# RWKV pairs in a hybrid trunk: products per head on 64x64 array parts, and the chunk inverse by 8x8 columns and doubling

## The chip, the cores and the metric

One core of a Trainium2 chip runs the whole program. Its engines work side by side, each through its own queue in order: TensorE (PE in the profile, with its weight loads as PEld), VectorE (DVE), ScalarE (ACT), GpSimd (POOL) and SyncE (SP, which issues the DMAs). The metric is the device time of one execution in microseconds (us). The kernel before takes 2580.99 us, the median of three runs (2580.29 to 2584.45).

## The reference

Two layers over 256 tokens of width 2048. Each adds a mixer and then a feed-forward part to the residual stream. Layer 0 mixes with HGRN2 and RWKV7, layer 1 with mLSTM and Mamba2. The change touches the RWKV7 part alone, 16 heads of 64 channels:

```
def rwkv7_scan(r, w, k, v, kk, a):
    def step(state, inp):
        rt, wt, kt, vt, kkt, at = inp
        sa = jnp.einsum('bhvk,bhk->bhv', state, -kkt)
        state = (state * wt[:, :, None, :] + sa[..., :, None] * (kkt * at)[:, :, None, :]
                 + vt[..., :, None] * kt[:, :, None, :])
        return state, jnp.einsum('bhvk,bhk->bhv', state, rt)
...
    o_rw = rwkv7_scan(rh, heads(decay), kh, vh, kk, heads(a))
    o_rw = head_layernorm(o_rw, rw_ln_w, rw_ln_b, RW_GN_EPS)
    bonus = (jnp.sum(rh * kh * rw_r_k, axis=-1, keepdims=True) * vh).reshape(b, s, RW_WIDTH)
    o_rw = (o_rw + bonus) * gate
```

The kernels don't step through tokens. They take chunks of 64: with the decays folded into the operands, a chunk's corrections `sa` for all its tokens solve a triangular system, so that the inverse of (I - M) is wanted, where M is a strictly triangular 64x64 matrix of products between the chunk's tokens, one for each head and chunk.

## The kernel before

The **large products** of all layers (the bulk) split each f32 operand in a high and a low part in a faster format and take three products of parts. `weights` (L275) loads a weight tile `raw`, ScalarE casts it to `whi` and VectorE subtracts to get `wlo`, with three tiles of each kind on chip. `bulk_a` (L293) has 512 columns moving, `bulk_b` (L319) 256. Both write to banks called `b`; all small products write to banks called `m`.

In **layer 0**, `flow` (L344) traces the bulk and, beside it, chains of small steps, as Python generators. In each round each active chain takes one step (two RWKV pairs and one HGRN2 head at a time), and then the bulk takes three steps (`EVEN_RATIO`), each of three to six products. What is traced in this order goes to the engines' queues, where the scheduler may still shift some of it. `ORDER` (L35) says in which order the bulk computes the inputs of the eight RWKV pairs and of HGRN2's parts, and the bulk of pair p waits until pair p - 3 is done (`AHEAD`). The chains' products have plain f32 operands; each such product is two instructions on TensorE in the profile. Transposes (`tr`, L135) are one.

A **pair** (`rwkv_pair`, L608) is two heads over four chunks of 64 tokens, all its tiles in one of two memory regions called `lane`. A matrix over a chunk's tokens that is a stationary operand stands block-diagonal, [128, 128] with the two heads' 64x64 blocks, half of it zero. VectorE makes those by masks (`masked`, L694; and `fh`, `sh` for B and K). In order, with a `yield` (the next step of the chain) between most of these:

- norms, decays and their exponentials; `vt` is v transposed for each chunk
- B and K block-diagonal, A and R side by side in `AR`
- `gram` (L687) twice: B and K as stationary operands against A and R, 128 columns moving; then `mt` copied by ScalarE, and the masks `m4`, `mrb`, `mak`, `mrk` by VectorE
- the inverse's diagonal blocks of 4 by Horner's rule (L719): three steps of four products with 4 columns moving. Between them `kt` (K transposed), `rv` and `o0` (products with v)
- four doublings, m = 4, 8, 16, 32 (L748): `halves` masks M's part (`lm`) and the inverse so far (`w`); TensorE transposes `w` and multiplies `lm` with x, ScalarE copies both results; in a second step TensorE multiplies them, and VectorE joins the halves. With m = 4 goes `kv`, with m = 8 `bt` (B transposed)
- the whole inverse made block-diagonal, transposed and copied to `xT`
- the scan over the four chunks, the only part whose products were per head before: `both` (L593) takes the two heads in turns on array parts of 64x64, at the lower and upper 64 partitions. The product with `xT` (L806) uses the full array
- layer norm, the transposes to `oc`, and the product with the gate

Of the kernel before, what the change touches and what calls it, by code (L numbers as in the profile page):

```python
# [16 lines left out]
ALU = mybir.AluOpType  # L17
# [8 lines left out]
# Blocks of 128 rows that a step over the weights takes, steps in one transfer and such transfers on chip where there  # L26
# is room for larger ones, and each kind of weight tile's number on chip.
# [13 lines left out]
PAIR_KB = dict(bon=0, AR=1, mrb=3, vt=4, B=5, K=7, mt=9, m4=11, mak=13, mrk=15, kt=17, kk=9, sqk=10, invw=11, k2=12,  # L41
               kka=13, b=14, E=15, rv=13, o0=15, kv=17, bt=5, lm=7, w=8, xh=11, y=14, x64=16, xw=9, xT=11, u=8, sq=7,
               oc=14)
PAIR_COL = dict(inv=0, gap=4, sm=8, var=12, x40=16, x41=32, x8=48, x16=80, x32=144, sd=272, st0=336, st1=400,
                rhs0=464, rhs1=528)
LANE = 19 * 256 + 592
# [16 lines left out]
class Arena:  # L63
    """Tiles that stay, one after the other in a few large ones."""
# [15 lines left out]
class Trunk:  # L80
# [42 lines left out]
    def rsqrt(self, x, scale, eps):  # L123
        """(x * scale + eps) ** -0.5 in place, for a few columns."""
        self.ts(x, x, scale, ALU.mult, eps, ALU.add)
        n = x.shape[-1]
        self.nc.gpsimd.tensor_tensor(out=x, in0=x, in1=self.nhalf[:, 0:n], op=ALU.pow)
# [29 lines left out]
    def even_masks(self, c):  # L157
# [5 lines left out]
        self.b4 = self.t(c, [P, P], "b4")  # L163
        for tl, m in ((self.bd, 64), (self.b4, 4)):
            nc.gpsimd.memset(tl, 1.0)
            self.same_block(tl.rearrange("p (j r) -> p j r", r=m), m, m)
        self.lev = {}
        for m in (1, 2, 4, 8, 16, 32, 64):
            nb = P // (2 * m)
# [6 lines left out]
        self.low = {}  # L176
        for m in (4, 8, 16, 32):
            tl = self.t(c, [P, 64 // m, m], f"low{m}")
            nc.gpsimd.memset(tl, 1.0)
            self.same_block(tl, 2 * m, m, m)  # L180
            self.low[m] = tl

    def even_masks_2(self, c):
        nc = self.nc
        self.upi = self.t(c, [P, 2, 64], "upi")
        self.ups = self.t(c, [P, 2, 64], "ups")
        self.up4 = self.t(c, [P, 2, 64], "up4")
        flat = lambda x: x.rearrange("p h t -> p (h t)")
        self.mul(flat(self.upi), self.up, self.bd)
        self.sub(flat(self.ups), flat(self.upi), self.ident)  # L190
        self.mul(flat(self.up4), flat(self.ups), self.b4)
        red = lambda o, x: nc.vector.tensor_reduce(out=o, in_=x, axis=AX.X, op=ALU.add)
        self.id4 = self.t(c, [P, 4], "id4")
        red(self.id4, self.ident.rearrange("p (j n) -> p n j", n=4))
        self.half_upi = self.t(c, [P, 64], "hupi")
        nc.vector.tensor_copy(out=self.half_upi[0:64], in_=self.upi[0:64, 0, :])
        nc.vector.tensor_copy(out=self.half_upi[64:128], in_=self.upi[64:128, 1, :])
        # 1 on the first (second) halves of blocks of 2m, as columns
        self.fh, self.sh = {}, {}
        for m in (4, 8, 16, 32, 64):  # L200
            f, g = self.t(c, [P, 1], f"fh{m}"), self.t(c, [P, 1], f"sh{m}")
            red(f, self.lev[m])
            self.ts(f, f, 1.0 / m, ALU.mult)
            self.ts(g, f, -1.0, ALU.mult, 1.0, ALU.add)
            self.fh[m], self.sh[m] = f, g
# [69 lines left out]
    def weights(self, src):  # L275
        """Parts of WK blocks of 128 rows of src [rows, n, c]: hi and lo as [128, WK, n * c]."""
# [7 lines left out]
    def weights_ahead(self, src, n, pool):  # L284
        """As weights, for n * WK blocks of src [rows, c] that come in one transfer."""
# [1056 lines left out]
```

## Time and profile before

| | |
|---|---|
| median of three runs | 2580.99 us |
| the profiled execution's span | 2578.8 us (nothing is profiled around it) |
| the pairs' chains, first to last | pair 0 begins at 123 us, pair 7 ends at 703 us |
| instructions of TensorE | 13969 |
| traffic with HBM | 424.35 MB read, 165 GB/s over the span |

The page of the profile gives each engine's busy time and its share of the span. Behind it stand views by stretch of time (windows), by line and form of instruction, the chain of waits that ended last, and the timeline of each engine. In the operands, `128*64` is the part of the array that a product uses, rows by columns, and `128x4` what moves through it. A matmul's end is modelled, so prices are read from one start to the next.

### The profile page before, as it was taken

The numbers are of one execution on the slowest core, as the hardware profiler recorded it, in microseconds if no ns is written. First come the engines' busy times: TensorE is split into PE (matmuls) and PEld (weight loads), VectorE is DVE, ScalarE is ACT, GpSimd is POOL, SyncE is SP. The second block draws the span as 40 slices with busy tenths as digits, with TensorE's granted clock in tenths as the row PEclk, the third lists the DMA queues.
The fourth block names the chain that finished last, engine by engine and source line by source line (L and its number), as shares of the span: only waits on it lengthen the run. The fifth ranks groups of instructions, "written<-read, shape, count | busy, mean of one in ns | idle before, by whom it ended". The sixth has DMA issues, their size and how long they took to land.

```text
span 2578.8 us, 35284 instructions
## 1 busy us (share of the span) xinstructions
PE 2543.4 (99%) x13969; PEld 2166.6 (84%) x13969; DVE 1499.9 (58%) x2327; ACT 1191.1 (46%) x1651; POOL 51.0 (2%) x106
## 2 busy tenths in 40 slices
PE   7999999999999999999999999999999999999998
PEld 5898899988788888888888899988888888888886
DVE  3567767766664454545454678656654544455455
ACT  5456556543354434444344555454544434443443
POOL 2000000000000000000000000000000000000000
PEclk9999999998999999999999999999999999999999
DMA  4633533232465555555555465567455555555554
GB/s 147 180 104 110 148 100 99 76 113 82 151 217 181 195 189 192 190 189 187 196 189 187 119 185 149 164 178 238 155 183 193 194 190 188 192 185 194 195 182 145
DMA packets 271094, 428.75 MB, mean 166 GB/s; under 512 B 18363, under 2 KB 86193, under 8 KB 270801
## 3 DMA queue, kind: packets, MB, share of 16 engines
q1 hardware_dynamic: 270353, 425.45, 52.3%
q8 instruction: 110, 1.80, 0.3%
q10 hardware_dynamic: 576, 1.05, 0.1%
q14 instruction: 55, 0.45, 0.0%
HBM read 424.35 MB, written 2.10 MB: 165 GB/s over the span
## 4 chain that ended last, share of the span: by engine, by line
PE 96%; DVE 2%; ACT 1%; DMA 1%; issue 0%; POOL 0%; SPq 0%; POOLq 0%; ACTq 0%; DVEq 0%
PE b L130 84%; PE m L130 8%; PE m L135 3%; DVE wlo L109 1%; PE m L597 1%; DMA act<-x 0%; ACT whi L269 0%; DMA raw<-w_in_even 0%; ACT xs L121 0%; ACT act L121 0%; DVE xs L103 0%; DVE act L109 0%; DVE act L106 0%; DVE act L112 0%; DVE cy L112 0%
## 5 line engine op out<-in xcount | busy, mean ns | idle before, releaser
L130 PE MATMUL b<-whi,act 128*128 128x512 f32 x5376 | 1687.1, 392 | 0.6
L109 DVE TENSOR_TENSOR wlo<-raw,whi 128x1024 fp32r<-128x1024 f32 (+2 forms) x818 | 978.0, 1198 | 862.5 <-ACT whi L269 855.5
L269 ACT CAST whi<-raw 128x1024 fp32r<-128x1024 f32 (+2 forms) x818 | 839.3, 1027 | 1128.2 <-PE b L130 1059.0
L130 PEld LDWEIGHTS b<-whi,act 128*128 128x128 f32 x5376 | 1010.6, 188 | 210.2 <-DVE act L109 1.9
L130 PE MATMUL b<-wlo,act 128*128 128x512 f32 x2688 | 1049.0, 390 | 0.0
L130 PEld LDWEIGHTS b<-wlo,act 128*128 128x128 f32 x2688 | 505.8, 188 | 103.2 <-DVE wlo L109 0.5
L130 PE MATMUL b<-act,whi 128*128 128x256 f32 (+1 forms) x2048 | 394.6, 290 | 0.3 <-ACT act L269 0.3
L130 PEld LDWEIGHTS b<-act,whi 128*128 128x128 f32 (+1 forms) x2048 | 319.1, 191 | 3.1 <-ACT act L269 0.7
L130 PE MATMUL b<-act,wlo 128*128 128x256 f32 (+2 forms) x1024 | 291.9, 288 | 1.0 <-DVE wlo L109 0.7
L130 PEld LDWEIGHTS b<-act,wlo 128*128 128x128 f32 (+2 forms) x1024 | 194.0, 191 | 2.7 <-DVE wlo L109 1.9
L130 PEld LDWEIGHTS m<-lane 128*128 128x128 f32 (+2 forms) x1024 | 115.5, 183 | 14.4 <-issue 7.8
L130 PE MATMUL m<-lane 128*128 128x64 f32 (+10 forms) x1024 | 123.2, 257 | 0.4 <-ACT lane L770 0.3
L106 DVE TENSOR_TENSOR act<-act,b 128x512 f32<-128x512 f32 x96 | 62.2, 682 | 11.0 <-PE b L130 11.0
L121 ACT ACTIVATE he<-he 128x256 f32<-128x256 f32 (+1 forms) x120 | 47.6, 408 | 22.1 <-DVE he L109 19.1
L135 PE MATMUL m<-const,lane 128*64 128x128 f32 (+2 forms) x304 | 45.3, 272 | 0.8 <-DVE lane L103 0.8
L103 DVE TENSOR_TENSOR lane<-lane,masks 128x256 f32<-128x256 f32 (+1 forms) x72 | 32.3, 451 | 14.9 <-PE m L130 13.9
L130 PE MATMUL m<-he 128*128 128x64 f32 (+1 forms) x240 | 38.3, 280 | 1.1 <-DVE he L103 1.1
L121 ACT ACTIVATE sg<-b,rs 128x512 f32<-128x512 f32 x44 | 29.9, 688 | 19.9 <-PE b L130 19.8
L135 PEld LDWEIGHTS m<-const,lane 128*64 128x64 f32 (+2 forms) x304 | 32.3, 126 | 6.6 <-issue 2.1
L130 PEld LDWEIGHTS m<-he 128*128 128x128 f32 x240 | 32.3, 193 | 3.0 <-ACT he L121 1.3
L103 DVE TENSOR_TENSOR he<-he,act 128x128 f32<-128x128 f32 x128 | 32.3, 288 | 3.1 <-ACT he L121 2.8
L112 DVE SCALAR_TENSOR_TENSOR gu<-b,rs,sg 128x512 f32<-128x512 f32 x44 | 30.9, 743 | 0.0
(243 smaller groups left out, 1104.3 us busy)
## 6 DMA issues: line engine op xcount, KB each, us to landing
raw<-ffn_w_up SPq DMA_DIRECT2D x176, 1024.0 KB
raw<-ffn_w_down SPq DMA_DIRECT2D x88, 1024.0 KB
raw<-w_in_odd SPq DMA_DIRECT2D x88, 512.0 KB
raw<-w_in_even SPq DMA_DIRECT2D x192, 128.0 KB
raw<-w_in_even SPq DMA_DIRECT2D x32, 512.0 KB
raw<-w_in_even SPq DMA_DIRECT2D x64, 256.0 KB
raw<-w_out_even SPq DMA_DIRECT2D x32, 512.0 KB
raw<-w_out_odd SPq DMA_DIRECT2D x32, 512.0 KB
```

Of the source, the lines that this page charges most:

```text
L103: self.nc.vector.tensor_tensor(out=out, in0=a, in1=b, op=ALU.mult)
L106: self.nc.vector.tensor_tensor(out=out, in0=a, in1=b, op=ALU.add)
L109: self.nc.vector.tensor_tensor(out=out, in0=a, in1=b, op=ALU.subtract)
L112: self.nc.vector.scalar_tensor_tensor(out=out, in0=a, scalar=s, in1=b, op0=op0, op1=op1)
L121: self.nc.scalar.activation(out=out, in_=a, func=f, **k)
L130: self.nc.tensor.matmul(out, lhsT, rhs, start=start, stop=stop)
L135: self.nc.tensor.transpose(out=out, in_=in_, identity=self.ident[b:b + k, b:b + k])
L269: self.nc.scalar.copy(out=hi, in_=src)
L597: self.nc.tensor.matmul(out[s], lhsT[s], rhs[s], start=start, stop=stop)
```

## The change

Nothing outside `rwkv_pair`, its masks and its places in memory is changed. In a pair:

- B, K and all masked matrices are [128, 4, 64]: a head's block on its own 64 partitions, nothing block-diagonal. VectorE makes B and K by one product each in place of two; the mask products go over 256 columns in place of 512, but there are seven (three for the doublings, `lm8`, `lm16`, `lm32`, which `mt` and its later masks were before).
- All products of two heads go through `heads`, which is `both` for each chunk, on 64x64 parts. That holds for `gram`, `rv`, `o0`, `kv`, the doublings and the product with the inverse.
- `vt`, `bt`, `kt` and `oc` are turned by products with the identity on 64x64 parts (`turned`), two instructions each, where they were transposes. ScalarE copies each of the first three once, where `vt` and `bt` took two copies; VectorE reads `oc` from its bank.
- Horner's rule is gone. The diagonal blocks of 8 are folded to 8 columns by a reduction; VectorE's `stream_shuffle` spreads the entries of columns 1 to 6 in each block of 8 partitions, and six pairs of small products and sums build the inverse of all 8x8 blocks.
- Three doublings are left. X and its transpose Y stand on 32 columns; `nc.vector.transpose` turns 32x32 blocks on VectorE. Each doubling has two products, X through M's level, then that through Y; VectorE adds to X, transposes to Y, and widens Y to 64 columns by a mask.
- A pair has 28 yields in place of 31.

The core of the diff:

```
-        B, K = T("B", BD), T("K", BD)
-        for o, x in ((K, k2), (B, kka)):
-            for h, sel in enumerate((self.fh[64], self.sh[64])):
-                self.stt(o[:, :, h, :], V4(x), sel, V4(E), ALU.mult, ALU.mult)
+        B, K = T("B"), T("K")
+        self.mul(K, k2, E)
+        self.mul(B, kka, E)
...
+    def heads(self, out, lhsT, rhs):
+        for ch in range(4):
+            self.both(out[:, ch, :], lhsT[:, ch, :], rhs[:, ch, :])
...
+        def turned(x, tag):
+            ps = quarter()
+            for ch in C4:
+                for h in range(2):
+                    s = slice(h * 64, (h + 1) * 64)
+                    self.mm(ps[s, ch, :], x[s, ch, :], self.ident[s, s])
+            if tag is None:
+                return ps
+            o = T(tag, CM)
+            nc.scalar.copy(out=o, in_=ps)
+            return o
...
-        for i in range(3):
-            ps = self.bank()[:, 0:16].rearrange("p (c n) -> p c n", n=4)
-            for ch in C4:
-                self.mm(ps[:, ch, :], m4[:, ch, :], self.id4 if x is None else x[:, ch, :])
-            x = T(f"x4{i % 2}", (P, 4, 4))
-            self.add(x, ps, i4)
...
+        z = T("m8", (P, 4, 8))
+        nc.vector.tensor_reduce(out=z, in_=m8e.rearrange("p c (j n) -> p c n j", n=8), axis=AX.X, op=ALU.add)
+        sh, tmp = T("sh", (P, 6, 4, 8)), T("tmp", (P, 4, 8))
+        for n in range(1, 7):
+            nc.vector.stream_shuffle(out=sh[:, n - 1].rearrange("p c n -> p (c n)"), in_=z.rearrange("p c n -> p (c n)"),
+                                     mask=[i // 8 * 8 + n for i in range(32)])
+        rv = times_v(mak, "rv")
+        yield
+        for n in range(1, 7):
+            w = 7 - n
+            self.mul(tmp[:, :, 0:w], sh[:, n - 1, :, n + 1:8], z[:, :, n:n + 1].broadcast_to([P, 4, w]))
+            self.add(z[:, :, n + 1:8], z[:, :, n + 1:8], tmp[:, :, 0:w])
+        self.add(z, z, by4(self.id8))
+        o = times_v(mrk, "o0")
+        yield
...
-        for m in (4, 8, 16, 32):
-            lm, w = halves(m)
...
-            ps = self.bank()[0:64].rearrange("p (c t) -> p c t", t=P)
-            for ch in C4:
-                self.tr(ps[:, ch, :], w[:, ch, :])
-            xT = T("xh", (64, 4, P))
-            nc.scalar.copy(out=xT, in_=ps)
...
+        nc.vector.transpose(out=flat(X), in_=flat(Y))
+        widened()
+        Yf = Y64.rearrange("p c j n -> p c (j n)")
+        for m in (8, 16, 32):
+            if m == 8:
+                kv = times_v(kt, "kv")
+            yield
+            ps = self.bank()[:, 0:P].rearrange("p (c n) -> p c n", n=32)
+            self.heads(ps, mt[m], X)
+            y = T("y", (P, 4, 32))
+            nc.scalar.copy(out=y, in_=ps)
+            yield
+            ps = self.bank()[:, 0:P].rearrange("p (c n) -> p c n", n=32)
+            self.heads(ps, Yf, y)
+            if m < 32:
+                self.add(X, X, ps)
+                nc.vector.transpose(out=flat(Y), in_=flat(X))
+                widened()
             else:
...
-            self.mm(pu, xT[:, ch, :], rhs)
+            self.both(pu, Yf[:, ch, :], rhs)
```

TensorE's queue around the two steps of pair 0's second doubling (m = 8) before: `m_1554` and `m_1560` are the transposes of `w` and the products of `lm`, `b_` the bulk.

```order
L130 MATMUL b_1536<-act_105,whi_1538 128x256
L130 MATMUL b_1536<-act_104,wlo_1539 128x256
L135 MATMUL m_1554<-const_58,lane_106_621 64x128 x4
L130 MATMUL m_1560<-lane_106_621 64x8 x4
L130 MATMUL b_1535<-act_104,whi_1538 128x256
L130 MATMUL b_1535<-act_105,whi_1538 128x256
```

And pair 0's second doubling (m = 16) in the changed kernel; `m_1569` is M's level times X, two heads by four chunks.

```order
L130 MATMUL b_1551<-act_105,whi_1553 128x256
L130 MATMUL b_1551<-act_104,wlo_1554 128x256
L586 MATMUL m_1569<-lane_106_606 64x32 x8
L130 MATMUL b_1550<-act_104,whi_1553 128x256
L130 MATMUL b_1550<-act_105,whi_1553 128x256
```

The transposes have left TensorE's queue, and a stretch of eight products on 64x64 parts stands alone between bulk products.

VectorE's queue from pair 0's Gram products to its first doubling, before: `m_1316` and `m_1324` are the Gram banks, the rows with 128x16 the sums of Horner's steps, `wlo` the bulk's weights.

```order
L103 TENSOR_TENSOR lane_106_621<-m_1316,masks_105_599 128x512
L103 TENSOR_TENSOR lane_106_621<-m_1316,masks_105_599 128x256
L103 TENSOR_TENSOR lane_106_621<-m_1324,masks_105_599 128x512 x2
L106 TENSOR_TENSOR lane_106_621<-m_1356,masks_105_599 128x16
L103 TENSOR_TENSOR lane_106_621<-lane_106_621,masks_249 128x256
L109 TENSOR_TENSOR wlo_1482<-raw_1480,whi_1481 128x1024
L106 TENSOR_TENSOR lane_106_621<-m_1393,masks_105_599 128x16
L109 TENSOR_TENSOR wlo_1539<-raw_1537,whi_1538 128x2x384
L106 TENSOR_TENSOR lane_106_621<-m_1430,masks_105_599 128x16
```

The same place in the changed kernel (`m_1302`, `m_1316` are the Gram banks now):

```order
L103 TENSOR_TENSOR lane_106_606<-m_1302,masks_105_593 128x256 x5
L103 TENSOR_TENSOR lane_106_606<-m_1316,masks_105_593 128x256 x2
L716 TENSOR_REDUCE lane_106_606<-lane_106_606 128x32
L719 STREAM_SHUFFLE lane_106_606<-lane_106_606 128x32 x6
L103 TENSOR_TENSOR lane_106_606<-lane_106_606 128x4x6
L106 TENSOR_TENSOR lane_106_606<-lane_106_606 128x4x6
L103 TENSOR_TENSOR lane_106_606<-lane_106_606 128x4x5
L106 TENSOR_TENSOR lane_106_606<-lane_106_606 128x4x5
L103 TENSOR_TENSOR lane_106_606<-lane_106_606 128x4x4
L106 TENSOR_TENSOR lane_106_606<-lane_106_606 128x4x4
```

Between these steps VectorE no longer takes results of TensorE: all of it follows from the Gram banks, one instruction after the other, with no weight tile of the bulk between them.

More of the change, by code (lines that the diff above doesn't have):

```diff
@@ L38 @@
 ODD_RATIO = 3.0
[L41 to L46, printed above, removed]
+PAIR_KB = dict(bon=0, AR=1, mrb=3, vt=4, u=4, B=5, rv=5, K=6, o0=6, kk=7, bt=7, k2=8, kt=8, sq=8, kka=9, mak=9, oc=9,
+               E=10, mrk=10, sqk=11, invw=11, m8e=11, Y=11, b=12, lm8=12, lm16=13, lm32=14, kv=15, X32=16, Y32=16.5,
+               y=17)
+PAIR_COL = dict(inv=0, gap=4, sm=8, var=12, m8=16, tmp=48, sh=80, sd=272, st0=336, st1=400, rhs0=464, rhs1=528)
+LANE_KB = 17.5
+LANE = int(LANE_KB * 256) + 592
 EPS = 1e-6
@@ L175, in even_masks, with fold @@
             self.lev[m] = tl
-        self.low = {}
-        for m in (4, 8, 16, 32):
[L178 to L181, printed above, removed]
     def even_masks_2(self, c):
         nc = self.nc
[L185 to L205, printed above, removed]
+        up = self.t(c, [P, P], "up2")
+        def fold(tag, x, n):
+            o = self.t(c, [P, n], tag)
+            nc.vector.tensor_reduce(out=o, in_=x.rearrange("p (j n) -> p n j", n=n), axis=AX.X, op=ALU.add)
+            return o
+        self.mul(up, self.up, self.bd)
+        self.upi = fold("upi", up, 64)
+        self.sub(up, up, self.ident)
+        self.ups = fold("ups", up, 64)
+        self.mul(up, up, self.b8)
+        self.up8 = fold("up8", up, 64)
+        self.lev64 = {m: fold(f"lev64_{m}", self.lev[m], 64) for m in (8, 16, 32)}
+        self.id8 = fold("id8", self.ident, 8)
+        self.m8, self.m32 = fold("m8", self.e8, 4), fold("m32", self.e32, 2)
     def same_block(self, v, size, keep, first=0):
@@ L525, in even_layer @@
             self.masks()
-            self.even_masks(Arena(self.t(masks, [P, 1664], "masks")))
+            self.even_masks(Arena(self.t(masks, [P, 1428], "masks")))
             self.omu = self.t(self.const, [P, 27], "omu")
@@ L602, in pair_tile @@
     def pair_tile(self, lane, tag, shape=(P, S)):
[L603 removed]
+        at = int(PAIR_KB[tag] * 256) if tag in PAIR_KB else int(LANE_KB * 256) + PAIR_COL[tag]
         v = lane[0:shape[0], at:at + math.prod(shape[1:])]
@@ L684, in rwkv_pair @@
         yield
-        Bf, Kf, ARf = flat(B), flat(K), flat(AR)
+        B, K = V4(B), V4(K)
+        ARf = AR.rearrange("p c h t -> p c (h t)")
         def gram(lhs):
-            ps = self.bank().rearrange("p (c h t) -> p c h t", c=4, h=2)
-            for ch in C4:
-                self.mm(ps[:, ch].rearrange("p h t -> p (h t)"), lhs[:, ch, :], ARf[:, ch, :])
-            return ps[:, :, 0, :], ps[:, :, 1, :]
+            ps = self.bank().rearrange("p (c n) -> p c n", n=P)
+            self.heads(ps, lhs, ARf)
+            return ps[:, :, 0:64], ps[:, :, 64:128]
         def masked(x, mask, tag):
-            o = T(tag, BD)
-            self.mul(o, wide(x), each(mask))
-            return flat(o)
+            o = T(tag, CM)
+            self.mul(o, x, by4(mask))
+            return o
         def times_v(lhs, tag):
             ps = quarter()
-            for ch in C4:
-                self.mm(ps[:, ch, :], lhs[:, ch, :], vt[:, ch, :])
+            self.heads(ps, lhs, vt)
             o = T(tag, CM)
@@ L705, in times_v @@
             return o
-        pm, pr = gram(Bf)
-        mt, mrb = T("mt", BD), T("mrb", CM)
-        nc.scalar.copy(out=mt, in_=wide(pm))
-        m4 = masked(pm, self.up4, "m4")
-        self.mul(mrb, pr, self.half_upi.unsqueeze(1).broadcast_to(list(CM)))
-        pm, pr = gram(Kf)
+        pm, pr = gram(B)
+        m8e = masked(pm, self.up8, "m8e")
+        mt = {m: masked(pm, self.lev64[m], f"lm{m}") for m in (8, 16, 32)}
+        mrb = masked(pr, self.upi, "mrb")
+        pm, pr = gram(K)
@@ L738, in halves @@
-        def halves(m):
-            nb = 64 // m
-            by = lambda mask: mask.unsqueeze(1).broadcast_to([P, 4, nb, m])
-            half = lambda v: v[..., m:2 * m]
-            lm, w = T("lm", (P, 4, nb, m)), T("w", (P, 4, nb, m))
-            self.mul(w, x.unsqueeze(2).broadcast_to([P, 4, nb, m]), by(self.low[m]))
-            self.mul(lm, half(mt.rearrange("p c h (j r) -> p c (h j) r", r=2 * m)),
-                     by(half(self.lev[m].rearrange("p (j r) -> p j r", r=2 * m))))
-            return (v.rearrange("p c j r -> p c (j r)") for v in (lm, w))
@@ L836, in rwkv_pair @@
         oc = T("oc")
-        ps = self.bank()[0:64].rearrange("p (c h t) -> p c h t", c=4, h=2)
-        for ch in C4:
-            self.tr(ps[:, ch, :, :].rearrange("p h t -> p (h t)"), o[:, ch, :])
-        for h in range(2):
-            nc.scalar.copy(out=V4(oc)[h * 64:(h + 1) * 64], in_=ps[:, :, h, :])
-        self.ts(oc, oc, col("ln_w"), ALU.mult, col("ln_b"), ALU.add)
+        self.ts(V4(oc), turned(o, None), col("ln_w"), ALU.mult, col("ln_b"), ALU.add)
         self.add(oc, oc, bon)
```

81 lines of the change are left out of this document (20 added, 61 removed).

## The prediction

> **What bounds the kernel now.** I read the page first, for the busy shares; then the windows of the layer that the change touches; then the chain of waits there; then TensorE's timeline at single places, for prices. The page's first part has one engine at its limit:
>
> ```profile
> PE 2543.4 (99%) x13969; PEld 2166.6 (84%) x13969; DVE 1499.9 (58%) x2327; ACT 1191.1 (46%) x1651; POOL 51.0 (2%) x106
> ```
>
> The pairs' chains run beside the large products of layer 0, from about 110 to 703 us. In the windows the columns are the stretch, its length, then busy time and instructions of PE, PEld, DVE, ACT and POOL, the granted TensorE clock, DMA share and GB/s; the last row below is of layer 1. Behind them stands the chain of waits from 100 to 745 us by line.
>
> ```profile
> 110.00:703.00 593.00, 590.05 (x4580) 533.05 (x4580) 422.06 (x1094) 298.83 (x584) 27.17 (x24) 0.97 0.39 111
> 150.00:300.00 150.00, 149.91 (x1134) 133.25 (x1133) 114.14 (x306) 89.89 (x178) 7.09 (x6) 1.00 0.40 114
> 550.00:600.00 50.00, 49.26 (x349) 42.41 (x348) 33.44 (x96) 21.03 (x43) 4.55 (x4) 0.80 0.27 83
> 580.00:585.00 5.00, 4.92 (x27) 4.37 (x27) 2.21 (x7) 1.87 (x6) 0.08 (x1) 0.50 0.01 3
> 1550.00:1600.00 50.00, 49.74 (x415) 48.92 (x413) 44.24 (x90) 26.00 (x37) 0.00 (x0) 1.00 0.47 137
> ```
>
> ```profile
> by line: PE b L130 60.7%; PE m L130 25.3%; PE m L135 5.9%; PE m L597 3.2%; DVE wlo L109 1.3%; issue 0.7%; ACT whi L269 0.5%; DVE act L106 0.4%; POOL lane L127 0.3%; DVE act L109 0.2%; DVE he L103 0.2%; DVE lane L831 0.2%; DVE lane L103 0.1%
> ```
>
> PE is busy for 590 of 593 us and holds some 95% of the chain; VectorE is busy for 422 (71%). So here a chain product costs its TensorE time in full, since the bulk stands behind it in the same queue. A busy PE is a modelled one, so prices are taken from start to start in the timeline, not from the mean durations. And the clock was 0.97 on the mean: 0.03 x 593 = **18 us** went to stretches at half clock (580 to 585: 0.50 while PE counts as busy for 4.92 of 5).
>
> **TensorE prices.** Timeline of PE; columns: start, time to the group's end, line, tiles, array part, moving operand, instructions. An f32 product is two instructions, so `both` for two heads is four.
>
> ```profile
> 676.76 0.39 PE L130 MATMUL b<-whi,act 128*128 128x512 f32 x1
> 677.08 0.33 PE L597 MATMUL m<-lane 64*64 64x64 f32 x4
> 677.34 0.50 PE L130 MATMUL b<-whi,act 128*128 128x512 f32 x1
> 677.68 0.39 PE L130 MATMUL b<-wlo,act 128*128 128x512 f32 x1
> 677.91 0.62 PE L130 MATMUL b<-whi,act 128*128 128x512 f32 x2
> ```
>
> ```profile
> 679.29 0.39 PE L130 MATMUL b<-whi,act 128*128 128x512 f32 x1
> 679.61 0.56 PE L597 MATMUL m<-lane 64*64 64x64 f32 x12
> 680.10 0.50 PE L130 MATMUL b<-whi,act 128*128 128x512 f32 x1
> 680.44 0.39 PE L130 MATMUL b<-wlo,act 128*128 128x512 f32 x1
> ```
>
> ```profile
> 682.05 0.40 PE L130 MATMUL b<-whi,act 128*128 128x512 f32 x1
> 682.28 0.33 PE L130 MATMUL m<-lane 128*128 128x64 f32 x2
> 682.42 0.47 PE L130 MATMUL b<-whi,act 128*128 128x512 f32 x1
> 682.74 0.39 PE L130 MATMUL b<-wlo,act 128*128 128x512 f32 x1
> ```
>
> A bulk product is 0.23 (677.68 to 677.91). From 676.76 to 677.68 stand two of them and one `both`: 0.92 - 0.46 = 0.46. From 679.29 to 680.44 stand two and three `both`: 1.15 - 0.46 = 0.69. So a further `both` is (0.69 - 0.46) / 2 = **0.115**, and a stretch of 64x64 work costs 0.46 - 0.115 = **0.345** to enter and leave, whatever it holds. A block-diagonal product on the full array is 0.69 - 0.46 = **0.23**, with no such toll. Half price per product, a toll per stretch: that is the trade of this change.
>
> [...]
>
> The inverse as it is: the third Horner step (8 instructions with 4 columns moving) with the 16 instructions of `rv` and `o0` (64 columns) that follow it in the queue, merged into one row; and one doubling level (m = 16) in its two steps.
>
> ```profile
> 144.32 2.79 PE L130 MATMUL m<-lane 128*128 128x4 f32 x24
> 146.91 0.48 PE L130 MATMUL b<-act,whi 128*128 128x256 f32 x2
> 147.24 0.28 PE L130 MATMUL b<-act,wlo 128*128 128x256 f32 x1
> ```
>
> ```profile
> 161.81 0.60 PE L135 MATMUL m<-const,lane 128*64 128x128 f32 x4
> 162.34 0.64 PE L130 MATMUL m<-lane 128*64 128x16 f32 x8
> 162.91 0.50 PE L130 MATMUL b<-act,whi 128*128 128x256 f32 x2
> 163.25 0.28 PE L130 MATMUL b<-act,wlo 128*128 128x256 f32 x1
> 163.37 0.40 PE L130 MATMUL b<-act,whi 128*128 128x256 f32 x2
> ```
>
> ```profile
> 164.69 0.28 PE L130 MATMUL b<-act,wlo 128*128 128x256 f32 x1
> 164.90 1.06 PE L130 MATMUL m<-lane 64*128 64x16 f32 x8
> 165.89 0.50 PE L130 MATMUL b<-act,whi 128*128 128x256 f32 x2
> 166.23 0.28 PE L130 MATMUL b<-act,wlo 128*128 128x256 f32 x1
> ```
>
> A 128x256 product is 0.12 (163.25 to 163.37). The 24 instructions: 2.92 - 0.24 = 2.68, **0.112** each; with the sixteen at 0.115, the eight of 4 columns take (2.68 - 1.84) / 8 = 0.105, so the width hardly sets it. The level: 1.44 - 0.24 = 1.20 and 1.54 - 0.36 = 1.18, together 2.38; its four transposes alone 0.53.
>
> For the Gram products, the chain of waits has all 16 instructions of a pair in one piece:
>
> ```profile
> 133.19 1.78 PE m L130 x16
> ```
>
> **Part 1, TensorE work for one pair.** Removed: Horner, 24 instructions in three steps, 24 x 0.112 = 2.69; four levels 4 x 2.38 = 9.52; `rv`, `o0`, `kv`, 24 instructions x 0.112 = 2.69; the four products with the inverse 4 x 0.23 = 0.92; Gram 1.78; the transposes of `vt`, `kt`, `xT`, `oc` 4 x 0.53 = 2.12; those of `bt`, eight on 64x64 parts in two stretches, at 0.46 each 0.92. Sum 20.64. Put in, in two-head products: three levels of eight, 24 x 0.115 = 2.76; `rv`, `o0`, `kv` 12 x 0.115 = 1.38; the inverse 4 x 0.115 = 0.46; `vt`, `bt`, `kt`, `oc` as products with the identity 16 x 0.115 = 1.84; Gram 8 products with 128 columns moving. These no row shows: at least 0.115 each, at most 4 x 0.111 = 0.445 (the heads one after the other). I take 0.222, each head's two instructions at the 0.111 of the row, the heads side by side as at 677.08: 1.78. Sum 8.22. The levels' products have 32 columns moving; 0.058 is their lower bound (half of 0.115), 0.115 is taken, since 4 columns cost as much as 64. Saved: 12.42, times 8 pairs = **-99 us**. Bounds: -11 us more (24 x 0.057 x 8) and 14 us less (8 x 0.223 x 8).
>
> **Part 2, the toll.** In the order of the built programs, TensorE enters a stretch of 64x64 products 57 times before (and 16 times for `bt`, priced above), 163 times after: 106 x 0.345 = **+37 us**. The 0.53 and 2.38 above hold their own changes of array part already.
>
> **Part 3, VectorE and ScalarE.** Groups by form; columns: operands, count, busy us, mean ns, idle time before.
>
> ```profile
> L103 DVE TENSOR_TENSOR lane<-m,masks 128x512 f32<-128x512 f32 x24 | 15.8, 684 | 1.2 <-ACT lane L708 0.9
> L103 DVE TENSOR_TENSOR lane<-lane,masks 128x512 f32<-128x512 f32 x8 | 5.5, 683 | 0.0
> L103 DVE TENSOR_TENSOR lane<-lane,masks 128x256 f32<-128x256 f32 x64 | 26.8, 422 | 14.9 <-PE m L130 13.9 <-PE m L135 0.4
> L112 DVE SCALAR_TENSOR_TENSOR lane<-lane,masks 128x256 f32<-128x256 f32 x32 | 13.9, 480 | 0.0
> L106 DVE TENSOR_TENSOR lane<-m,masks 128x16 f32<-128x16 f32 x24 | 4.2, 174 | 12.7 <-PE m L130 12.6
> L103 DVE TENSOR_TENSOR he<-he,act 128x128 f32<-128x128 f32 x128 | 32.3, 288 | 3.1 <-ACT he L121 2.8
> ```
>
> These first four go: 62.0 / 8 = 7.8 us a pair, with three adds of 16 columns (0.5) and eight joins of 16 to 128 columns between 0.174 and 0.288 (1.8): 10.1. Added: eleven passes over 256 columns and a reduction over 256, 12 x 0.422 = 5.1; three passes of 128 columns, 0.86; 13 small ones x 0.174 = 2.3; six shuffles of 32 columns and five transposes of 128, which no row shows, between 0.174 and 0.422 each (1.9 to 4.6), taken by the nearest width, 6 x 0.174 + 5 x 0.288 = 2.5. Sum 10.7: about nothing, +0.6 a pair.
>
> [...]
>
> But VectorE must do this in less time: (422 + 5) / (593 - 62) = 80%. And part of it moves into one place: from the Gram products to the first level stand 7 masks, the reduction, 6 shuffles, 13 small steps, a pass of 128 and one of 256 columns and a transpose: 2.95 + 0.42 + 1.04 + 2.26 + 0.29 + 0.42 + 0.29 = 7.7 us in one chain. The old way needed three masks of 512 columns, `mrb`, three adds and the first level's two passes: 2.05 + 0.42 + 0.52 + 0.84 = 3.8. If nothing hid the other 3.9 us, TensorE would wait 8 x 3.9 = 31 us. What hides it is the bulk: between two steps of a lane the order keeps up to 18 bulk products (2.2 us), and in 150 to 300 us VectorE is idle for 24%. In layer 1 VectorE is busy for 44.24 of 50 and PE still for 49.74, so 88% can do without waits. I take **+8 us**, between 0 and 31. ScalarE loses copies and stands at 50%: nothing.
>
> **Part 4, the clock.** The half clock of 580 to 585 stands where TensorE counts as busy, so it is not idleness alone that brings it; I take it that narrow products do, such as Horner's with 4 columns. They go; what comes in has 32 or more. That link is a guess, which is why only half is counted. But steps without bulk beside them get shorter, and TensorE may idle there instead. Between -18 (gone) and 0, and above nothing if it spreads (a rival); taken: **-9 us**.
>
> Sum: -99 + 37 + 8 - 9 = -63 (-63.8 unrounded, with 99.4 and 36.6). The profiled span is 2578.8 us, 2.2 below the median of 2581.0: 2515 in the profile's terms, **2517 us** in the runs'.
>
> **Rivals.** (a) All goes well: no waits, no half clock, 32 columns at the lower bound: -63 - 18 - 11 = -92, 2489; without the last, 2500. For it: TensorE's 3 idle us in 593. Chance 0.12. (b) The saved work comes back as waiting: VectorE's longer chain is not hidden (+31), and the idle spots bring 5 us more of half clock than now. With Parts 1 and 2 that is -99 + 37 + 31 + 5 = -26, **2555**. For it: 80% on VectorE, in one queue with the weights' split; against it, the layer 1 row. Chance 0.20. (c) Slower: each stretch arrives before its operands. TensorE takes its queue in order, so it holds the bulk behind it. 163 stretches x w: it decides at w = 63.8 / 163 = 0.39 us, and at 0.8 us gives -64 + 130 = +66, 2647. For it: a chain step's TensorE time halves while the bulk between steps stays, so results are wanted sooner. Against it: the same steps now cost 3 idle us in all. Chance 0.04. (d) The change does not shorten what bounds, no change: it would take a layer bound by something else, and 590 of 593 speaks against it. Chance 0.02.
>
> **The numbers.** The forecast, 0.62, has its own range of 2500 to 2540. The range to hold 8 in 10 takes in most of (a) and reaches (b): **2492 to 2556**. A measurement of this kernel can tell about 0.2% (5 us) from no change. Faster by more: 0.62 + 0.12 + 0.20 less a little = 0.93; within: 0.03; slower: 0.04.
>
> **What would show it.** Right: layer 0 some 60 us shorter, everything behind it the same; in the timeline, a stretch of eight 64x64 products between bulk at about 0.345 + 4 x 0.115 = 0.81; Gram at 0.22 a product; PE still busy for nearly all of the layer, VectorE at 80%. Wrong: a toll away from 0.345, Gram at 0.44, waits of PE on `lane` tiles of VectorE in tens of us, or longer stretches with a clock of 0.5.

## The result and the profile after

The changed kernel takes 2512.07 us, the median of four runs (2511.5 to 2523.66), against 2582.72 for the kernel before, run beside it (2580.29 to 2585.08): ratio 0.975, 95% interval [0.972, 0.978], -71 us. The forecast was 2517, in a range of 2492 to 2556.

Page of the profile after, its first part, and windows of it (the changed layer from 110 to 637 us, and a piece of it; columns as before):

```profile
PE 2471.2 (98%) x14609; PEld 2089.6 (83%) x14609; DVE 1492.2 (59%) x2462; ACT 1156.2 (46%) x1573; POOL 51.9 (2%) x100
```

```profile
110.00:637.00 527.00, 519.25 (x5219) 456.70 (x5218) 416.43 (x1242) 264.68 (x506) 29.95 (x24) 1.00 0.44 126
500.00:530.00 30.00, 27.46 (x373) 23.55 (x372) 24.03 (x86) 12.21 (x28) 2.99 (x3) 1.00 0.46 135
```

The layer's stretch is 527 us long where it was 593 (the large product that starts at 703 us before starts at 636 us here). TensorE still bounds it, but idles for 7.75 us (527 - 519.25) where it idled for 3. VectorE is busy for 79% (416.43 of 527), where 80% was expected. The granted clock is 1.00 throughout. The profiled span went from 2578.8 to 2510.9, so -67.9 us in the profiles.

Timeline of PE after: one group of 64x64 products (16 instructions, four two-head products) between bulk products, and the Gram products with `bt` and `kt`:

```profile
137.59 0.28 PE L130 MATMUL b<-act,wlo 128*128 128x256 f32 x1
137.80 0.68 PE L586 MATMUL m<-lane 64*64 64x64 f32 x16
138.41 0.50 PE L130 MATMUL b<-act,whi 128*128 128x256 f32 x2
138.75 0.28 PE L130 MATMUL b<-act,wlo 128*128 128x256 f32 x1
```

```profile
132.62 1.97 PE L586 MATMUL m<-lane 64*64 64x128 f32 x32
134.42 1.10 PE L130 MATMUL m<-const,lane 64*64 64x64 f32 x32
135.45 0.50 PE L130 MATMUL b<-act,whi 128*128 128x256 f32 x2
```

From 137.59 to 138.75 stand three bulk products of 0.12 and the group: 1.16 - 0.36 = **0.80** us, where 0.345 + 4 x 0.115 = 0.81 was forecast. The Gram products take 134.42 - 132.62 = 1.80, forecast 1.78.

The waits of PE from 60 to 650 us, the largest two of a table (in total, times, longest, in us):

```profile
PE b L130 <- DVE wlo L109: 2.2, 5, 0.9
PE m L130 <- DVE lane L719: 1.0, 1, 1.0
```

No single wait is longer than 1.0 us, and most end on VectorE.

**The clock, for reading all that follows.** Some executions of most of these kernels spend 27.3 us more at half clock at about 46 to 74 us, ahead of the changed work, which costs them 13.6 us. The row below, of after_serial's profile, shows one; four more of the profiles have it. That executions of the kernel before and of the changed one have it too is told from their mean clock alone (the changed kernel's 0.993 against 0.998 and 0.999).

```profile
46.00:74.00 28.00, 28.00 (x67) 13.29 (x67) 4.57 (x19) 8.85 (x22) 0.00 (x0) 0.51 0.08 24
```

So beside each median stands the **time at full clock**: a run's span times its mean granted clock, the median over the runs. It is worked out, and holds as far as TensorE bounds the time. Between runs of one kernel it varies by up to 8 us.

| kernel | 64x64 stretches | median us | at full clock | clock of the runs |
|---|---|---|---|---|
| before (46 runs beside the experiments) | 73 | | 2559 | 0.986 to 0.998 |
| after | 163 | 2512.1 | 2505 | 0.993 to 0.999 |
| after_again (the same, later) | 163 | 2512.4 | 2504 | 0.993 to 0.999 |
| after_serial | 163 | 2536.7 | 2531 | 0.993 to 0.999 |
| after_split | 266 | 2568.4 | 2548 | 0.990 to 0.999 |
| after_extra | 180 | 2549.0 | 2526 | 0.991 to 0.993 |
| after_full | 87 | 2549.1 | 2529 | 0.990 to 0.996 |
| before_wide | 73 | 2565.3 | 2558 | 0.993 to 0.999 |
| after_dve | 163 | 2520.6 | 2514 | 0.992 to 0.999 |
| after_single | 115 | 2513.0 | 2498 | 0.990 to 0.997 |
| after_single2 | 115 | 2512.0 | 2498 | 0.989 to 0.997 |
| after_lock | 103 | 2517.5 | 2497 | 0.989 to 0.996 |
| after_a4r25 | 170 | 2537.5 | 2508 | 0.989 to 0.990 |
| after_single_a4 | 123 | 2522.7 | 2506 | 0.993 to 0.995 |

The kernel before, in the four groups of its runs beside the experiments, had medians of 2576 to 2580, and of 2559 to 2560 at full clock. What the clock costs it differs by execution: from 5 to 36 us over the 46 runs (span times one less the clock), so the 17 us of its profile are one case.

### The profile page after: what moved, and what is told of

Its sections match the earlier page's. It is cut to its first block, busy times and chain, and to the rows that moved or that the text cites. A ratio compares the mean times of both kernels' runs of the same rounds, so it can differ in the third digit from the quotient of the medians.

```text
span 2510.9 us, 36580 instructions
## 1 busy us (share of the span) xinstructions
PE 2471.2 (98%) x14609; PEld 2089.6 (83%) x14609; DVE 1492.2 (59%) x2462; ACT 1156.2 (46%) x1573; POOL 51.9 (2%) x100
## 4 chain that ended last, share of the span: by engine, by line
PE 94%; DVE 3%; ACT 1%; DMA 1%; issue 1%; POOL 0%; SPq 0%; POOLq 0%; ACTq 0%; DVEq 0%
PE b L130 85%; PE m L130 4%; PE m L586 3%; PE m L135 2%; DVE wlo L109 1%; DMA raw<-w_in_even 1%; ACT whi L258 0%; DMA act<-x 0%; ACT act L121 0%; DVE lane L103 0%; DVE act L109 0%; ACT xs L121 0%; ACT L121 0%; POOL lane L127 0%; DVE xs L103 0%
## 5 line engine op out<-in xcount | busy, mean ns | idle before, releaser
L586 PEld LDWEIGHTS m<-lane 64*64 64x64 f32 x1952 | 75.6, 134 | 30.9 <-issue 8.7
L586 PE MATMUL m<-lane 64*64 64x64 f32 (+2 forms) x1952 | 96.5, 232 | 1.3 <-DVE lane L738 1.0
L121 ACT ACTIVATE xs<-act 128x512 f32<-128x512 f32 x40 | 24.7, 620 | 11.9 <-DVE act L106 7.2
L109 DVE TENSOR_TENSOR act<-m,act 128x512 fp32r<-128x512 f32 x44 | 28.2, 682 | 0.0
```

Source lines behind the costliest of these rows:

```text
L109: self.nc.vector.tensor_tensor(out=out, in0=a, in1=b, op=ALU.subtract)
L121: self.nc.scalar.activation(out=out, in_=a, func=f, **k)
L586: self.nc.tensor.matmul(out[s], lhsT[s], rhs[s], start=start, stop=stop)
```

## The experiments

**1. Is it the heads side by side?** after_serial turns the loops of each group:

```diff
-        for ch in range(4):
-            self.both(out[:, ch, :], lhsT[:, ch, :], rhs[:, ch, :])
+        for h in range(2):
+            s = slice(h * 64, (h + 1) * 64)
+            for ch in range(4):
+                self.mm(out[s, ch, :], lhsT[s, ch, :], rhs[s, ch, :])
```

> The changed kernel with the order of each group of 64x64 products turned: first one head's four chunks, then the other head's, so that neighbours in TensorE's queue stand on the same array part. Same instructions, same 163 stretches. T1 (the gain is that two heads run side by side at half price): a two-head product goes from 0.115 back to about 0.224 us, 52 of them in a pair (0.109 x 52 = 5.7) and 8 Gram products from 0.222 to 0.444 (1.8), so 7.5 x 8 = +60 us, about 2572, nearly the whole gain. Rival T2 (the gain is the shorter inverse, fewer products; the order of the heads does not matter): 0, 2512.

Measured: 2536.7, at full clock +26 us, under half of what T1 said and far from T2's nothing. Its timeline, the same group of 16 instructions, and then the Gram products with `bt` and `kt`, which now run into each other:

```profile
149.63 0.28 PE L130 MATMUL b<-act,wlo 128*128 128x256 f32 x1
149.84 0.96 PE L130 MATMUL m<-lane 64*64 64x64 f32 x16
150.73 0.51 PE L130 MATMUL b<-act,whi 128*128 128x256 f32 x2
151.07 0.29 PE L130 MATMUL b<-act,wlo 128*128 128x256 f32 x1
```

```profile
143.97 2.24 PE L130 MATMUL m<-lane 64*64 64x128 f32 x29
...
147.50 0.50 PE L130 MATMUL b<-act,whi 128*128 128x256 f32 x2
```

The group takes 1.44 - 0.36 = 1.08 in place of 0.80, so +0.28, not the 4 x 0.109 = 0.44 that I had put. The Gram piece takes 147.50 - 143.97 = 3.53 in place of 2.83 (135.45 - 132.62): +0.70, where 8 x 0.109 for `bt` and `kt` and 1.8 for Gram were expected. The starts of single instructions tell why the turned order costs so little. The first 0.08 us of the Gram products, in the changed kernel and then in after_serial:

```profile
132.62 0.33 PE L586 MATMUL m<-lane 64*64 64x128 f32 x2
```

```profile
143.97 0.32 PE L130 MATMUL m<-lane 64*64 64x128 f32 x1
```

In the changed kernel the two heads' instructions start 0.006 us apart, and a new pair every 0.109 us (every 0.058 with 64 columns): side by side. In after_serial one head starts alone, but the other head's first instruction follows at 144.46, while the first head's go on to 144.78; from there on two series run interleaved. In the group of four the second head starts at 150.13, the first head's last instruction at 150.30. (Which head a start belongs to is read from the order of the queue; the trace doesn't name it.) So the edit did not put the heads fully one after the other, and the 26 us are a lower bound of what running side by side is worth. It doesn't test what Gram would cost without it.

**2. The toll by itself.** after_split and after_extra put the same full-array product into 104 groups, once in the middle and once at the end (`at` is 1 or 3; the products with the identity in `turned` likewise):

```diff
         for ch in range(4):
             self.both(out[:, ch, :], lhsT[:, ch, :], rhs[:, ch, :])
+            if ch == at and extra is not None:
+                self.mm(extra, self.ident, self.ident[:, 0:64])
```

> The changed kernel with one f32 product of identities on the full array (128 x 64 columns, into unused columns of the same bank, read by nobody) in the middle of 104 groups of 64x64 products, between the second and the third chunk: 266 stretches in place of 163. T1 (a toll of 0.345 for each stretch): 104 x 0.224 + 103 x 0.345 = 23 + 36 = +59 us, 2571. Rival (no toll, the 0.345 was waiting for operands): +23 us, 2535. To be held against after_extra.

> As after_split, but the product of identities stands behind the fourth chunk, at the end of the same 104 groups: 180 stretches. T1: 104 x 0.224 + 17 x 0.345 = 23 + 6 = +29 us, 2541, so 30 us below after_split (86 stretches fewer). Rival (no toll): +23 us, the same as after_split.

Measured at full clock: +43 and +21 us, 22 us apart. One group of each in the timeline, after_split first:

```profile
150.52 0.28 PE L130 MATMUL b<-act,wlo 128*128 128x256 f32 x1
150.73 0.45 PE L586 MATMUL m<-lane 64*64 64x64 f32 x8
151.10 0.44 PE L130 MATMUL m<-const 128*128 128x64 f32 x2
151.47 0.45 PE L586 MATMUL m<-lane 64*64 64x64 f32 x8
151.85 0.50 PE L130 MATMUL b<-act,whi 128*128 128x256 f32 x2
152.19 0.28 PE L130 MATMUL b<-act,wlo 128*128 128x256 f32 x1
```

```profile
149.85 0.28 PE L130 MATMUL b<-act,wlo 128*128 128x256 f32 x1
150.06 0.68 PE L586 MATMUL m<-lane 64*64 64x64 f32 x16
150.67 0.44 PE L130 MATMUL m<-const 128*128 128x64 f32 x2
150.92 0.48 PE L130 MATMUL b<-act,whi 128*128 128x256 f32 x2
151.24 0.28 PE L130 MATMUL b<-act,wlo 128*128 128x256 f32 x1
```

1.67 - 0.36 = 1.31 against 1.39 - 0.36 = 1.03: the same products, and 0.28 us more for leaving 64x64 work and entering it again, with nothing waited for. 86 stretches x 0.28 = 24 us, and 22 are measured. So the toll is real, in the queue itself; the rival (both the same) falls. It was 0.28 here, not 0.345. The two kernels also cost about 16 and 8 us less than T1 said. From 60 to 650 us TensorE idles for 2 us in after_split and for 3 in after_extra, in the changed kernel for 8: some of the added work filled waits.

**3. What the packing is worth in all.** after_full keeps the new inverse and does the groups on the full array:

```diff
         for ch in range(4):
-            self.both(out[:, ch, :], lhsT[:, ch, :], rhs[:, ch, :])
+            c0 = min(ch * 64, 128)
+            self.mm(out[:, ch, :], lhsT.rearrange("p c t -> p (c t)")[:, c0:c0 + P], rhs[:, ch, :])
```

> The changed kernel with its new inverse, its masks and its copies, but each group of two-head products (Gram, rv, o0, kv, the levels, the products with the identity) done as four products on the full array. The stationary operand takes the next 64 columns as the other head's, so the block structure is left out and the values are not the reference's; the amount and order of work are those of a block-diagonal version without its wider masks. 87 stretches of 64x64 in place of 163. T1 (half price and a toll nearly cancel in groups of four: after_serial's and the profile's rows give 0.80 us for such a group packed and 0.92 on the full array): 416 x 0.112 dearer = +47, 76 x 0.335 of toll less = -25, Gram the same: +21, less up to 10 that waits give back as in after_extra: 2523 to 2533. So packing would be worth some 10 to 20 of the 70 us, and the inverse the rest. Rival T3 (packing is the gain, tolls hidden): +47 or more, 2559.

Measured: +24 us at full clock, near T1's +21 (with nothing given back by waits) and half of T3's; in the median +37 (2549.1), outside T1's range. The clock is the difference: its profile has the early stretch, and in this layer two stretches of 6.8 us at half clock, 6.8 us lost, that the changed kernel has not. (Their windows, 531.7 to 538.5 and 569.3 to 576.1, have a clock of 0.50.) The group in its timeline:

```profile
149.53 0.28 PE L130 MATMUL b<-act,wlo 128*128 128x256 f32 x1
149.66 1.00 PE L130 MATMUL m<-lane 128*128 128x64 f32 x8
150.46 0.48 PE L130 MATMUL b<-act,whi 128*128 128x256 f32 x2
150.78 0.28 PE L130 MATMUL b<-act,wlo 128*128 128x256 f32 x1
```

1.25 - 0.36 = 0.89 for four products on the full array, 0.80 packed: half price and toll nearly cancel where a stretch holds four. Of the 54 us that the change brings at full clock (2559 to 2505), the packing is 24, and the other 30 is the rest of it; that this is the shorter inverse above all is argued from Part 1, not tested by itself. With the clock lost in this layer the packing is about 31 of the 68 us between the profiles. That split flatters the inverse a little or the packing not enough, since after_full does without the wider masks that a true block-diagonal version needs.

**4. The half clock.** before_wide is the kernel before with wider moving operands, the products' number and order unchanged (the first product of each doubling level and the second alike):

```diff
+        rep = lambda v: v.unsqueeze(1).broadcast_to([v.shape[0], 64 // v.shape[1], v.shape[1]])
...
-                self.mm(ps[:, ch, :], m4[:, ch, :], self.id4 if x is None else x[:, ch, :])
+                self.mm(ps[:, ch, :], m4[:, ch, :], rep(self.id4 if x is None else x[:, ch, :]))
```

> The kernel before, where the moving operand of the Horner products and of both products of a doubling level is repeated to 64 columns, of which only the first 4 to 32 are read afterwards. Same instruction count, same order. T1 (narrow products bring the half clock): no half clock between 518 and 604 us, granted clock there 1.00 and not 0.80, -17 us, less 1 to 5 for the wider products: 2567 to 2571. Rival (the half clock comes from TensorE's waits in the rounds without bulk, which stay): clock as before, +1 to +5 us, 2584 to 2588.

Measured: 2565.3 against 2579.7 beside it, ratio 0.996 [0.994, 0.998]; at full clock the same as before (2558 and 2559). So the same products, made wider, cost nothing and give back the clock. Windows of the profile of before at its three stretches of half clock, with the 3.4 us ahead of the first and the last; and TensorE's timeline at the last:

```profile
515.00:518.40 3.40, 2.29 (x21) 2.12 (x19) 2.60 (x9) 2.44 (x7) 0.00 (x0) 1.00 0.42 116
518.40:525.20 6.80, 6.80 (x35) 6.58 (x34) 2.46 (x8) 1.41 (x3) 0.00 (x0) 0.50 0.23 60
...
528.60:532.00 3.40, 3.40 (x23) 3.02 (x23) 2.08 (x8) 0.84 (x2) 0.00 (x0) 0.51 0.34 114
576.40:579.80 3.40, 3.40 (x31) 3.31 (x29) 1.27 (x6) 1.31 (x3) 0.00 (x0) 1.00 0.00 0
579.80:603.70 23.90, 23.49 (x94) 18.73 (x94) 12.79 (x34) 6.93 (x16) 2.70 (x2) 0.50 0.14 44
```

```profile
576.38 2.00 PE L130 MATMUL m<-lane 128*128 128x4 f32 x16
...
578.74 3.56 PE L130 MATMUL m<-lane 128*128 128x4 f32 x21
```

From 576.4 to 579.8 TensorE counts as busy for 3.40 of 3.40 us, with Horner's products of 4 columns and the products of 64 columns that stand between its steps, apart from two large products at 578.2 (the timeline merges both into one row by the first one's shape), and then the clock halves for 23.9 us. Half of 6.8 + 3.4 + 23.9 is 17 us lost. In before_wide the window of the last is:

```profile
560.00:605.00 45.00, 45.00 (x330) 38.52 (x329) 36.93 (x87) 20.16 (x40) 2.13 (x2) 1.00 0.33 107
```

From 560 to 605 us the kernel before has a clock of 0.73 on the mean. T1 holds for this kernel: its narrow products brought the half clock (made 64 columns wide, they left 1.00), even where TensorE counts as busy for 3.40 of 3.40 us. They were not the only way, as the next runs show.

**5. The lone products.** after_single puts 56 lone two-head products on the full array, on block-diagonal copies by ScalarE:

```diff
+        for wide, x in ((W, Yf), (btw, bt)):
+            for h in range(2):
+                self.act(wide[:, :, h, :], x, AF.Identity, scale=self.bd[:, h * 64:h * 64 + 1])
...
-            self.both(pu, Yf[:, ch, :], rhs)
+            self.mm(pu, W[:, ch, :], rhs)
...
-                self.both(pst, bt[:, ch, :], u[:, ch, :])
+                self.mm(pst, btw[:, ch, :], u[:, ch, :])
```

> The changed kernel with the two products that stand alone in their step (the inverse with the right-hand side, and B^T with u: 56 of them) put back on the full array, on block-diagonal copies that ScalarE makes with four activations a pair. 115 stretches in place of 163. T1 (a stretch costs 0.335 to 0.345 whatever it holds, so a lone two-head product at 0.455 loses against 0.225 on the full array): 56 x 0.11 = +6, 48 x 0.335 = -16, so -10 us, 2502. Rival (half price counts, the toll is waiting): +6 us, 2518.

Measured: at full clock -7 us, so T1's sign: more TensorE work per product and still less time. But the median is 2513.0, no better. The best runs (2508) lack the early stretch; even they lose 3.4 us to half clock that the changed kernel has not. Timeline of PE at the first such place, and windows around it:

```profile
235.57 0.43 PE L130 MATMUL m<-lane 128*128 128x64 f32 x2 [2.88 <-ACT lane L121]
```

```profile
233.20:236.60 3.40, 1.03 (x5) 0.90 (x6) 1.64 (x7) 3.23 (x6) 1.00 (x1) 1.00 0.33 124
236.60:240.00 3.40, 3.40 (x12) 2.83 (x11) 2.71 (x7) 0.71 (x2) 0.00 (x0) 0.50 0.18 38
```

The new copies made TensorE wait for 2.88 us, and right behind that it runs at half clock for 3.4 us. So here the half clock followed on a wait. Its stretches in these profiles last 3.4, 6.8, 23.9 and 27.3 us, multiples of 3.41. TensorE was not idle throughout ahead of them: it was busy for 1.03 of the 3.40 us shown here, and in the kernel before for all 3.40 ahead of the longest.

after_single2 moves the two copies of `bt` two levels earlier, to shorten that wait:

> after_single, where two of its four activations (the block-diagonal copy of B^T) stand two levels earlier, so that only the two for the inverse lie between the last transpose and the products that use them. Same 115 stretches. In after_single TensorE waited once 2.88 us for these activations (232.7 to 235.6) and ran at half clock for 3.4 us right behind it. T1 (toll saved, and the half clock comes from such a wait): that wait falls below 1.5 us, the half clock at 237 goes, and the time at full clock is 2 to 3 us below after_single's 2498: 2498 to 2503 in the runs without the early 27 us at half clock. Rival (ScalarE is short of time there in any case): wait and half clock stay, as after_single, 2508 to 2513.

Measured: nothing moved (2512.0; 2498 at full clock), and the wait is again 2.88 us; the rival holds. Timeline of ScalarE of after_single2 before the products' start at 235.09:

```profile
230.01 1.28 ACT L121 ACT_TABLE_LOAD   x1
...
232.74 1.28 ACT L121 ACT_TABLE_LOAD   x1
234.03 0.20 ACT L121 ACTIVATE lane<-lane 128x3 f32<-128x3 f32 x1
234.15 0.89 ACT L121 ACTIVATE lane<-lane,masks 128x256 f32<-128x256 f32 x2
```

The two copies for the inverse (0.89) stand in ScalarE's queue behind HGRN2's activations and two table loads of 1.28 us. Not the number of copies, but what stands ahead of them, makes the wait. Copies on VectorE or GpSimd weren't tried.

**6. Fewer stretches by locking the lanes.** after_lock queues the pairs by twos (with `AHEAD = 4` and `EVEN_RATIO = 2.7`):

```diff
-            self.put("rw", f"rw{p}", self.rwkv_pair(p, *(rkv[:, i, :] for i in range(3))))
+            ready.append((p, rkv))
+            if p % 2:
+                for q, x in ready[-2:]:
+                    self.put("rw", f"rw{q}", self.rwkv_pair(q, *(x[:, i, :] for i in range(3))))
```

> The changed kernel with the pairs' chains queued by twos, so that both lanes do the same step in the same round and their 64x64 products stand next to each other; four pairs' inputs may stand ready in place of three, and 2.7 steps of the stream go with a round in place of 3.0. 103 stretches in place of 163, same products. T1 (toll per stretch): -60 x 0.335 = -20 us, 2492, if VectorE's work, now bunched by twos, stays covered. Rival (VectorE bounds the chain's rounds): a round with both lanes' seven masks holds 5.8 us of VectorE; two or three such rounds in each of four batches each some 2 to 3 us short of cover, +16 to +36 against the toll's -20: 2508 to 2528.

Measured: -8 us at full clock (2497), none of it in the median (2517.5). Windows from 60 to 650 us, of after and then of after_lock:

```profile
60.00:650.00 590.00, 582.25 (x5528) 509.83 (x5527) 452.15 (x1302) 294.19 (x545) 29.95 (x24) 1.00 0.46 134
```

```profile
60.00:650.00 590.00, 573.85 (x5530) 510.42 (x5529) 446.90 (x1302) 291.72 (x541) 24.55 (x24) 0.99 0.45 134
430.70:434.10 3.40, 1.29 (x9) 1.18 (x10) 3.40 (x13) 1.58 (x5) 0.00 (x0) 1.00 0.00 0
```

TensorE idles for 8.4 us more, so of -20 some 12 are left, of which 8 came. The half clock takes as much again: its profile has four stretches, 17 us together, so 8.5 lost. At 430.7 to 434.1 VectorE is busy for all 3.40 us and TensorE for 1.29, and half clock follows. Both theories had a part: the toll is saved, and VectorE, bunched, gives much of it back.

**7. VectorE's chain.** after_dve repeats the shuffles of a pair four times:

```diff
-        for n in range(1, 7):
+        for n in [*range(1, 7)] * 4:
             nc.vector.stream_shuffle(
```

> The changed kernel with each of the six shuffles of a pair done four times (18 more at 0.185 us, 3.3 us a pair in the chain between Gram and the first level, where I counted 3.9 us of longer VectorE chain). T1 (the stream's products behind each step cover most of VectorE's chain): between 0 and +8 us, 2512 to 2520, VectorE 84% busy. Rival (VectorE's chain is exposed in the changed kernel): +3.3 x 8 = +27 us, 2539.

Measured: 2520.6 and at full clock +9 us, just over T1's upper end and a third of the rival's +27. So a microsecond added to that chain costs about a third of one: it is covered mostly, not wholly.

**8. The rounds without stream products.** after_a4r25 has `AHEAD = 4` and `EVEN_RATIO = 2.5`; after_single_a4 adds them to after_single.

> The changed kernel with four pairs' inputs ready in place of three and 2.5 steps of the stream in a round in place of 3.0, so that no round of the chains is left without stream products (seven are now, at about 500 to 530 us, where TensorE is idle for 2.5 of 30 us). 170 stretches in place of 163. T1 (what the sum lacked are waits in those rounds): -5 to -10 us with +2 for the stretches, 2504 to 2509. Rival (VectorE, 90% busy from 530 to 565 us, bounds the late rounds whatever stands beside them): 0, 2510 to 2515, with the waits in other places.

> after_single with the same two settings as after_a4r25: 123 stretches. T1: the two add up, -7 (after_single at full clock) and -3 to -8, so 2497 to 2502, and the half clock of after_single at 237 and 537 us (3.4 us each) goes where its waits go. Rival: only the -7 of the fewer stretches, 2505.

Both miss: at full clock +3 and +1 us against after, in the medians +25 and +11 (13.6 of the 25, by its profile, are the early stretch). Two windows of after_a4r25:

```profile
500.00:530.00 30.00, 29.99 (x413) 26.99 (x412) 25.22 (x92) 11.61 (x28) 1.84 (x2) 1.00 0.56 156
174.20:177.60 3.40, 1.39 (x17) 1.04 (x17) 3.17 (x14) 1.93 (x4) 0.00 (x0) 1.00 0.00 0
```

At 500 to 530 us TensorE's idle time is gone (29.99 busy), as T1 said. But with fewer stream products in each round it now idles elsewhere, as at 174 to 178 us beside a VectorE that is busy for 3.17 of 3.40, and the clock halves behind it (0.54 on the mean from 177 to 184 us). The rival holds.

**9. The spread.** after_again is the changed kernel once more:

> The changed kernel once more, unaltered, beside after_single2 on the same chip, for the spread: 2510 to 2513 where the clock is 0.998 or above, about 2524 where the early 27 us at half clock strike.

Measured: 2512.4 (2510.7 to 2523.2), as before. None of the variants beats it in the median by more than the spread.

## Why the prediction was right

By the profiles, -67.9 us came where -63.8 was forecast. The clock is -17 of it (the half clock of 518 to 604 us, all gone), and TensorE's work with its waits the other -51, where Parts 1 to 3 had -54.8.

- **The bound.** Right: TensorE bounds the layer before and after, and the added work of the runs above showed in the time, less what filled waits.
- **Part 1, products.** The prices held: 0.80 for a group (forecast 0.81), 1.80 for Gram (1.78). A group with 32 columns moving, read in the same way at 146.68 us, costs 0.77, so the levels' lower bound was rightly not taken. The reason given for Gram, the heads side by side, held too (starts 0.006 us apart, a pair every 0.109). But Parts 1 and 2 together brought too little. TensorE's busy time fell by 72.2 us (2543.4 to 2471.2), 17 of it the clock, so its work fell by 55 where -99.4 + 36.6 = -62.8 was forecast. Some 1.6 us of those 8 are the transposes of `kt` and `xT`, counted at the 0.53 of the levels' narrower ones: four on the full array take 0.43 (573.95 to 574.74 in the kernel before, 0.79 less three products of 0.12), so 2 x 0.10 x 8. The rest stays open.
- **Part 2, toll.** The largest doubt of the sum, and shown: 163 stretches, 0.28 us for one more (after_split), and a lone product is cheaper on the full array (after_single). The price read from before, 0.345 beyond the products, gives the group's 0.80 rightly; taken as the cost of one more entry into an existing group it is a little high.
- **Part 3, waits.** +8 was forecast between 0 and 31. Idle time rose by 4.8 us (7.75 against 2.95), a little less than taken; the 8 us that TensorE's work lacks are not in it. Of the prices that no row showed, a shuffle took 0.185 us (0.174 taken), a transpose 0.303 to 0.306 (0.288), the reduction 0.636 (0.422). after_dve's third, on the 31 us of longer chain, would give about 10, an estimate.
- **Part 4, the clock.** The link to narrow products, put as a guess, was right, and only its size off: -17 where half, -9, was counted. before_wide shows it (1.00 from 560 to 605 us, where the kernel before has 0.73). That these 8 us more and the 8 us that Parts 1 and 2 lack cancel is luck; without it the total would not be as near as 4 us.
- **The rivals.** (a) had the clock right, and no waits, which came. (b) fell: no half clock came back, and VectorE's chain is exposed by a third, not wholly. (c) fell: 7.75 us of waits over 163 stretches is 0.05 each, against the 0.39 from which it decides. (d) fell.

What the title of the change names first, the 64x64 parts, is less than half of it: 24 of 54 us at full clock, about 31 of 68 with the clock. The price of a product was halved with 64 columns moving (0.115 against 0.23), but not with Gram's 128 (1.80 against 1.78 for a pair's), and the toll took back most in the groups of four (0.80 against 0.89).

## What to carry to other kernels

Price a packed product as a stretch: what it costs to enter and leave (0.28 to 0.345 us here) and then the product (0.115); a lone one lost against the full array (0.46 against 0.23), four gained a tenth (0.80 against 0.89), and an estimate from these prices has only longer stretches get near half; with 128 columns moving there was nothing to gain. The kernel before, which TensorE bounds, lost clock to its own narrow products while TensorE counted as busy (17 us of its profile), so read the granted clock beside the busy share, by stretch; repeating the operand to 64 columns cost nothing here (2558 against 2559 us at full clock) and gave the clock back. When an edit saves TensorE work, look at each wait that it makes: behind one of 2.88 us stood 3.4 us at half clock, 1.7 us more.

## What the hardware showed that was not expected

- Two heads' products on 64x64 parts ran side by side (starts 0.006 us apart), and TensorE began the second head's also where all of the first head's stood ahead of them in the queue (150.13 against 150.30). So the order of the heads cost a group of four 0.28 us (0.80 to 1.08), and not 0.44.
- The half clock followed on windows of different kinds: full of products of 4 and 64 columns without a gap (3.40 of 3.40 us busy), with one wait of 2.88 us, with several waits (1.29 of 3.40 busy). By a count, what they share is few columns moving. In the kernel before, the stretches at half clock begin at 518.4, 528.6 and 579.8 us and last 6.8, 3.4 and 23.9; their lengths and distances are multiples of 3.41 us (61.4 from the first to the last is 18 of them). So all fourteen profiles were divided from 60 to 700 us into pieces of 3.41 us, on whose edges the clock's changes fall, and in each piece at full clock the moving columns of all product instructions that start in it were added up. In the kernel before, the three pieces ahead of half clock had 2200, 1568 and 1788 columns (the last, ahead of the longest stretch, in 28 instructions), and no other had fewer than 2592; in the changed kernel, with no half clock there, none had fewer than 3072. Over the fourteen, each of the 14 pieces with fewer than 2000 columns was followed by half clock; with 2000 to 2832 columns, 6 of 16; with more, none of 2537 (the median piece has 5900). This is a count, not a test: some records can be missing from a trace, and of the experiments before_wide alone changed the columns and nothing else.
- The early stretch of 27.3 us at half clock, from about 46 us, comes in some executions and not in others of the same kernel. In the five profiles that have it, the piece of 3.41 us ahead of it had 2304 to 2560 columns; in the nine others no piece that begins between 40 and 60 us had fewer than 2816. That fits the count above. Why it comes in some executions and not in others, no run shows.
